# Value products of an attention pair grouped one stage later, and the operands of TensorE gathered at the low SBUF addresses

## The chip, the cores and the metric

One core of a Trainium2 chip runs the whole program: TensorE for matmuls, VectorE (DVE), ScalarE (ACT) and GpSimd (POOL) for the rest, SyncE (SP) for the queue of most transfers. The metric is the device time of one execution in microseconds, here the median of three runs.

## What is computed

A network of three blocks over a sequence of 512 positions and 1024 features, in float32:

```python
a = rmsnorm(h, g); q, k, v, u, z = split(a @ w_in)
h = h + rmsnorm(concat(norm(dilated_attention(q, k, v)), norm(gating(u, z))) @ w_out, g)   # 8 heads
h = h + rmsnorm((silu(f @ w_gate) * (f @ w_up)) @ w_down, g)                              # 2816 wide
h = h + sigmoid(h @ w_pe_gate + b) * (p @ w_pe_proj)
for i in range(2):
    h = rms_norm(x) * (1 + sc1) + sh1
    mix = stick_breaking_attention(h) if i == 0 else dsa_attention(h)                     # 16 heads each
    x = x + g1 * mix
    x = x + g2 * conv_ffn(rms_norm(x) * (1 + sc2) + sh2)                                  # 2816 wide
```

All three attentions end alike: a 512 x 512 matrix of weights per head, lower triangle only, times the head's values (512 x 64). `dsa_attention` first picks 128 keys per query by an index score.

## The kernel before

Activations are kept feature-major: 128 features on the partitions, 512 positions along the row, so a tensor of 1024 features is eight tiles of 128 x 512. Every large product is made of three: each operand is rounded to a `float32r` high part and a low part that holds the remainder, and `mm3` (L103) adds low weights x high operand, high weights x high operand, high weights x low operand into one PSUM bank. `unit` (L82) loads 128 x 1024 weights into `raw` and rounds them into two pairs `whi`, `wlo` (ScalarE casts, VectorE subtracts); the streamed operands are `hh`/`hl` (normed activations), `mh`/`ml`, `q` or `k` (attention outputs before their projection) and `Hh`/`Hl` (22 tiles each, the inner layer of a feed-forward part). In a product of 128 x 128 weights and a 128 x 512 operand the operand is the moving one; only the values (`tokmajor`) do it the other way round.

The program runs in order: the dilated mixer with its gating (`mixer_a`), a feed-forward part with a gate (`ffn_a`), stick-breaking attention (`mixer_sb`), a feed-forward part (`ffn_conv`), sparse attention (`mixer_dsa`), a second `ffn_conv`.

Attention is written out by hand in `attend` (L522). It goes through pairs of heads, 4 in the first part and 8 in each of the other two, with one stage per pair. In stage i it issues eight `block`s (scores and weights of pair i+1, one for each head and block of 128 queries) and, for pair i, `tr` after every second block and `mul` behind it; between them it takes a number of steps from `filler`, a generator of float32r products that have nothing to do with the pair (projections to come). While `order` is on, TensorE runs its instructions exactly in the order written (`queue`, L71).

`av` (L636) makes the three functions of a pair. `tr(kb)` turns the weights of key block kb, 128 columns at a time, into the PSUM tile `tt` (one buffer), and copies it to `AT` (two buffers). `mul(kb)` multiplies it with the values `v`, for both heads, into bank `po` (one buffer), in full float32 on 64 columns of the array: four records in the profile. In the stage, `mul(kb-1)` follows `tr(kb)`, and `mul(3)` and `end` close it. `end` rounds `po` into the operand of the output projection (`ms`).

SBUF tiles live in pools that are laid out one behind the other from the low end: `const`, `w` (raw, whi, wlo, ada), `x` (X, hh, hl), `small` (acc, sq, R and others, 8608 bytes), then the pools of the stage that runs. A tile takes its size rounded up to 32 bytes per partition.

Of the kernel before, what the change touches and what calls it, by code (L numbers as in the profile page):

```python
# [8 lines left out]
F32 = mybir.dt.float32  # L9
F32R = mybir.dt.float32r  # L10
# [44 lines left out]


class K:
    def __init__(self, tc, a, stop=99):
# [5 lines left out]
    def t(self, pool, shape, dt=F32, tag="t", bufs=None):  # L64
        self.n += 1
        return pool.tile(list(shape), dt, name=f"{tag}_{self.n}", tag=tag, bufs=bufs)


# [18 lines left out]
    def unit(self, src, widths=(512, 512), eng=None):  # L87

        nc = self.nc
        n, raw = sum(widths), src  # L90
        if src is not self.first:
            raw = self.t(self.wp, [P, UNIT], F32, "raw", bufs=4)
            nc.sync.dma_start(raw[:, :n], src[:, :n])
        out, c = [], 0
        for w in widths:
            hi = self.t(self.wp, [P, 512], F32R, "whi", bufs=7)
            lo = self.t(self.wp, [P, 512], F32R, "wlo", bufs=7)
            nc.scalar.copy(hi[:, :w], raw[:, c:c + w])  # L98
# [11 lines left out]
    def units(self, srcs):  # L110

        nc = self.nc
        raws, out = [], [[] for _ in srcs]
        for src in srcs:
            raws.append(self.t(self.wp, [P, UNIT], F32, "raw", bufs=4))
            nc.sync.dma_start(raws[-1], src)
        for j in range(2):
            for raw, o in zip(raws, out):
                hi = self.t(self.wp, [P, 512], F32R, "whi", bufs=7)
                lo = self.t(self.wp, [P, 512], F32R, "wlo", bufs=7)  # L120
# [149 lines left out]
    def build(self):  # L270
        tc, nc, a = self.tc, self.nc, self.a
        with ExitStack() as ctx:
            cp = ctx.enter_context(tc.tile_pool(name="const", bufs=1))
            self.wp = ctx.enter_context(tc.tile_pool(name="w", bufs=1))
            self.xp = ctx.enter_context(tc.tile_pool(name="x", bufs=1))
            self.sp = ctx.enter_context(tc.tile_pool(name="small", bufs=1))
            self.dp = ctx.enter_context(tc.tile_pool(name="dram", bufs=1, space=bass.MemoryType.DRAM))
            self.pp = ctx.enter_context(tc.tile_pool(name="banks", bufs=1, space=PSUM))
            self.cp = cp

            X = [self.t(self.xp, [P, S], F32, f"X{k}") for k in range(KD)]
            self.consts = self.t(cp, [P, NCOLS], F32, "consts")
# [7 lines left out]
            self.order(False)  # L290
            self.ident = self.t(cp, [P, P], F32, "ident")
            nc.gpsimd.memset(self.ident, 0.0)
# [43 lines left out]
    def mixer_a(self, X, raw):  # L336
# [9 lines left out]
        with ExitStack() as ctx:  # L346
            mp = ctx.enter_context(tc.tile_pool(name="mixa", bufs=1))
            gctx = ctx.enter_context(ExitStack())
# [108 lines left out]

            def av(i, A):
                o, tr, mul = self.av(at, A, lambda kb, h: V[kb][:, (2 * i + h) * 64:(2 * i + h + 1) * 64], nc.scalar.copy)

                def end():
                    if i < 2:
# [60 lines left out]
    def attend(self, pairs, block, av, filler, budget, ahead=0):  # L523

        A = None
        self.order(True)
        for _ in range(ahead):  # L530
            next(filler, None)
        for i in range(-1, pairs):
            nxt, n = [[], []], budget[i + 1]
            share = (0, 2, 3, 4, 5, 6, 7, 8, 9)
            if i >= 0:
                tr, mul, end = av(i, A)
            for s in range(8):
# [12 lines left out]
        for _ in filler:  # L550
            pass
        self.order(False)

# [81 lines left out]

    def av(self, pool, A, V, copy):  # L636

        nc = self.nc  # L640
        out, at = self.bank("po"), {}
# [13 lines left out]

        def mul(kb):
            for h in range(2):
                self.matmul(out[h * 64:h * 64 + 64, kb * P:], V(kb, h), at[kb][:, h, :S - kb * P], start=kb == 0, stop=kb == NB - 1)

# [232 lines left out]
    def mixer_sb(self, X):  # L892
        tc, nc, a = self.tc, self.nc, self.a
        with tc.tile_pool(name="sb", bufs=1) as mp:
            w = a["sb_w_in"]
            slab, operand = self.enter(X, 0, [w[8 + i] for i in range(4)])
            identb = self.t(mp, [P, P], BF16, "identb")
            nc.vector.tensor_copy(identb, self.ident)
            dmask = self.t(mp, [P, S], F32, "keep", bufs=2)[:, :P]
            nc.vector.memset(dmask, 0.0)  # L900
# [27 lines left out]
            def block(h, qb):  # L928
# [15 lines left out]
            def av(i, A):  # L944
                o, tr, mul = self.av(mp, A, lambda kb, h: V[kb][:, (2 * i + h) * 64:(2 * i + h + 1) * 64], None if i == 7 else nc.vector.tensor_copy)

                def end():
                    if i < 6:
                        ms.append(self.split(o, i, "m", mp))
                        return  # L950
# [26 lines left out]
    def ffn_conv(self, X, l):  # L977
        tc, nc, a = self.tc, self.nc, self.a
        with tc.tile_pool(name="ffn", bufs=1) as fp:
            w = a["ffn_w_up"][l]  # L980
# [32 lines left out]
    def mixer_dsa(self, X):  # L1013
        tc, nc, a = self.tc, self.nc, self.a
        with ExitStack() as ctx:
            Tw = self.Tw
            mp = ctx.enter_context(tc.tile_pool(name="dsa", bufs=1))
            w = a["dsa_w_in"]
# [24 lines left out]
            self.slabs([pk[:72]], [self.unit(w[5], (288, 288))], xs, m=72)  # L1043
            ki = self.t(mp, [P, 1, 2, S], F32R, "AT", bufs=2)
            for h in range(2):
# [88 lines left out]
            def ahead():  # L1134
# [16 lines left out]
                nc.vector.tensor_mul(gg, self.col("dsa_q_norm"), self.col("dsa_k_norm"))  # L1151
                kn.append(self.t(mp, [P, S], F32, "kn"))
                nc.vector.scalar_tensor_tensor(kn[0], lat, gg, Rk, op0=ALU.mult, op1=ALU.mult)
# [83 lines left out]
            def av(i, A):  # L1237
                o, tr, mul = self.av(mp, A, lambda kb, h: V[kb][:, (2 * i + h) * 64:(2 * i + h + 1) * 64], nc.scalar.copy)

                def end():  # L1240
                    hi = self.t(mp, [P, S], F32R, f"q{2 * i}")
                    lo = self.t(mp, [P, S], F32R, f"q{2 * i + 1}")
# [23 lines left out]
    def rel_bias(self, pool):  # L1266
# [3 lines left out]
        nc.gpsimd.dma_start(rb, a["rel_bias"])  # L1270
        row = self.t(pool, [P, 2, S], F32, "AT", bufs=2).rearrange("p a b -> p (a b)")[:DH]
        b = t5_buckets()
# [101 lines left out]
```

## Time and profile before

| | us |
|---|---|
| median of three runs | 1953.95 (1952.02 to 1954.26) |
| the profiled execution | 1953.02 |
| its span | 1951.3 |
| TensorE busy | 1912.0 |
| VectorE busy | 1297.6 |
| ScalarE busy | 906.4 |
| GpSimd busy | 366.4 |

The span runs from the first to the last instruction. Busy times of one engine count overlapping records once. Matmuls are pipelined, so that a record of TensorE is longer than the time by which it delays the next one; the distance between two starts tells that. A granted clock of 1.00 is TensorE's upper level, 2.4 GHz. Names such as `mm<-hh,wlo` are the tile written and the two tiles read.

### The profile page before, as it was taken

The numbers are of one execution on the slowest core, as the hardware profiler recorded it, in microseconds if no ns is written. First come the engines' busy times: TensorE is split into PE (matmuls) and PEld (weight loads), VectorE is DVE, ScalarE is ACT, GpSimd is POOL, SyncE is SP. The second block draws the span as 40 slices with busy tenths as digits, with TensorE's granted clock in tenths as the row PEclk, the third lists the DMA queues.
The fourth block names the chain that finished last, engine by engine and source line by source line (L and its number), as shares of the span: only waits on it lengthen the run. The fifth ranks groups of instructions, "written<-read, shape, count | busy, mean of one in ns | idle before, by whom it ended". The sixth has DMA issues, their size and how long they took to land.

```text
span 1951.3 us, 24100 instructions
## 1 busy us (share of the span) xinstructions
PE 1912.0 (98%) x8610; PEld 1504.1 (77%) x8610; DVE 1297.6 (66%) x2354; ACT 906.4 (46%) x1672; POOL 366.4 (19%) x348
## 2 busy tenths in 40 slices
PE   7999799999999999999999999999999999999999
PEld 6887678888887787767888888886665688888887
DVE  6686775556356666776888874568967677666431
ACT  5365443223324455554544443345588655444321
POOL 3020331111000302332111110013454221111000
PEclk8999899999999999999999999999999999999999
DMA  5232156555464243222366555522212123322331
GB/s 181 87 89 69 62 170 188 192 184 177 144 219 148 79 129 87 76 63 81 105 204 198 196 170 167 212 92 98 81 60 65 33 89 119 97 98 95 94 108 49
DMA packets 70382, 236.93 MB, mean 121 GB/s; under 512 B 8085, under 2 KB 8677, under 8 KB 70262
## 3 DMA queue, kind: packets, MB, share of 16 engines
q1 hardware_dynamic: 69556, 234.47, 37.4%
q8 instruction: 67, 1.10, 0.2%
q10 hardware_dynamic: 578, 0.85, 0.2%
q14 instruction: 53, 0.43, 0.1%
q0 software_dynamic: 128, 0.08, 0.0%
HBM read 226.87 MB, written 2.21 MB: 117 GB/s over the span
## 4 chain that ended last, share of the span: by engine, by line
PE 88%; DVE 8%; issue 2%; ACT 1%; POOL 1%; DMA 0%; SPq 0%; POOLq 0%; DVEq 0%; ACTq 0%
PE mm L81 52%; PE sc L81 27%; PE po L81 5%; PE tt L84 2%; PE tt L81 1%; DVE isc L1093 1%; DVE m L1092 1%; DVE hl L262 1%; DVE wlo L99 0%; DVE hh L589 0%; DVE X L590 0%; DVE g L739 0%; DVE wlo L123 0%; DVE hl L852 0%; DVE v L1030 0%
## 5 line engine op out<-in xcount | busy, mean ns | idle before, releaser
L98 ACT CAST whi<-raw 128x512 fp32r<-128x512 f32 (+1 forms) x550 | 327.5, 607 | 423.5 <-PE mm L81 248.9
L99 DVE TENSOR_TENSOR wlo<-raw,whi 128x512 fp32r<-128x512 f32 (+1 forms) x518 | 381.6, 745 | 206.2 <-ACT whi L98 201.8
L81 PE MATMUL mm<-hh,wlo 128*128 128x512 f32 (+1 forms) x1000 | 406.4, 406 | 3.5 <-ACT hh L261 3.5
L81 PE MATMUL mm<-hl,whi 128*128 128x512 f32 x1032 | 402.1, 393 | 0.0
L81 PE MATMUL mm<-hh,whi 128*128 128x512 f32 (+1 forms) x1000 | 391.9, 392 | 0.0
L81 PEld LDWEIGHTS mm<-hh,wlo 128*128 128x128 f32 (+1 forms) x1000 | 188.6, 189 | 70.9 <-issue 30.3
L81 PEld LDWEIGHTS mm<-hl,whi 128*128 128x128 f32 x1032 | 194.4, 188 | 42.3
L767 DVE CUSTOM_DVE_ANT_0 ada<-ada,bc 128x1024 f32<-128x1024 f32 x112 | 139.8, 1248 | 124.0 <-DMA ada<-in_ada_w 96.5
L81 PEld LDWEIGHTS mm<-hh,whi 128*128 128x128 f32 (+1 forms) x1000 | 188.7, 189 | 36.4 <-issue 0.8
L81 PE MATMUL sc<-hh,wlo 128*128 128x512 f32 x416 | 162.5, 391 | 0.0
L81 PE MATMUL sc<-hl,whi 128*128 128x512 f32 x416 | 162.3, 390 | 0.0
L81 PE MATMUL sc<-hh,whi 128*128 128x512 f32 x416 | 162.3, 390 | 0.0
L190 POOL TENSOR_TENSOR acc<-acc,sq 128x512 f32<-128x512 f32 x53 | 84.9, 1601 | 407.1 <-ACT sq L195 399.5
L81 PE MATMUL mm<-Hl,whi 128*128 128x512 f32 x364 | 144.3, 397 | 0.0
L81 PE MATMUL mm<-Hh,wlo 128*128 128x512 f32 x364 | 144.1, 396 | 0.0
L81 PE MATMUL mm<-Hh,whi 128*128 128x512 f32 x364 | 143.6, 395 | 0.0
L1004 POOL TENSOR_TENSOR g<-g,u 128x512 f32<-128x512 f32 x44 | 62.6, 1422 | 413.5 <-DVE u L1000 358.6
L252 ACT CAST Hh<-g 128x512 fp32r<-128x512 f32 x66 | 41.0, 621 | 164.3 <-POOL g L691 100.7
L81 PEld LDWEIGHTS sc<-hh,wlo 128*128 128x128 f32 x416 | 78.5, 189 | 16.3
L81 PEld LDWEIGHTS sc<-hh,whi 128*128 128x128 f32 x416 | 78.4, 189 | 16.3
L81 PEld LDWEIGHTS sc<-hl,whi 128*128 128x128 f32 x416 | 78.4, 188 | 16.3
L81 PE MATMUL sc<-Hl,whi 128*128 128x512 f32 x220 | 87.4, 397 | 0.0
(364 smaller groups left out, 3356.0 us busy)
## 6 DMA issues: line engine op xcount, KB each, us to landing
ada<-in_ada_w SPq DMA_DIRECT2D x96, 512.0 KB, 4.0
raw<-in_ffn_w_up SPq DMA_DIRECT2D x88, 512.0 KB, 3.2
raw<-in_w_gate_up SPq DMA_DIRECT2D x44, 512.0 KB, 4.3
raw<-in_ffn_w_down SPq DMA_DIRECT2D x32, 512.0 KB, 3.5
raw<-in_sb_w_in SPq DMA_DIRECT2D x24, 512.0 KB, 3.2
raw<-in_dsa_w_in SPq DMA_DIRECT2D x21, 512.0 KB, 3.4
raw<-in_w_in SPq DMA_DIRECT2D x19, 512.0 KB, 3.3
raw<-in_w_down SPq DMA_DIRECT2D x16, 512.0 KB, 4.1
```

Of the source, the lines that this page charges most:

```text
L81: self.queue(self.nc.tensor.matmul(*args, **kw))
L84: self.queue(self.nc.tensor.transpose(*args))
L98: nc.scalar.copy(hi[:, :w], raw[:, c:c + w])
L99: (eng or nc.vector).tensor_sub(lo[:, :w], raw[:, c:c + w], hi[:, :w].bitcast(F32))
L190: (eng or self.nc.gpsimd).tensor_add(acc, acc, self.square(src))
L252: self.nc.scalar.copy(hi, src)
L262: self.nc.vector.scalar_tensor_tensor(lo, src, col, hi.bitcast(F32), op0=ALU.mult, op1=ALU.subtract)
L767: nc.vector.tensor_tensor_reduce(raw, raw, row, scale=1.0, scalar=0.0, op0=ALU.mult, op1=ALU.add, accum_out=out))
L1004: nc.gpsimd.tensor_mul(g, g, u)
L1092: nc.vector.max(m8, work[qb][:, :L])
L1093: nc.vector.match_replace(work[qb][:, :L], m8, work[qb][:, :L], SENT)
```

## The change

Five things change.

`attend` no longer issues `mul` and `end` in the stage of their pair. It keeps them as `late` and issues all four `mul` and `end` in the next stage, behind its first block; those of the last pair come behind the rest of the filler. `tr` stays where it was. `AT` becomes four tiles, one per key block and of its size; in the dilated part the one of 256 columns borrows the tile `bc`. The bank `po` is taken at `mul(0)`.

Pools get a side. From the low end come `unit` (ident), `wt` (whi, wlo) and `x` (hh, hl); from the high end `const`, `w` (raw, ada), `res` (the residual X) and `small`. A stage's pool becomes two (`Homes`): the tags named go to the low side, all others to the high side. Low are the operands `mh`/`ml`, `qs`, `k` in the dilated and stick-breaking parts, `q` and the `v` tags in the sparse part, and in the feed-forward parts all `Hh` and `Hl8` to `Hl11`.

`norms` in the sparse part squares two heads at a time and issues their two products together, with one copy instead of two.

`keep` in the stick-breaking part uses the tiles `R` and `acc` in turn instead of two of its own; `kn` in the sparse part uses `acc`.

The tile for the mask, the index keys and the bias row is `AT512` instead of `AT`.

```diff
+class Homes:
+    def tile(self, shape, dt, name, tag, bufs=None):
+        return (self.low if tag in self.tags else self.high).tile(shape, dt, name=name, tag=tag, bufs=bufs)
...
+    @contextmanager
+    def homes(self, name, tags):
+        with self.tc.tile_pool(name=name, bufs=1) as low, self.tc.tile_pool(name=name + "_", bufs=1, side="right") as high:
+            yield Homes(low, high, tags)
...
-            hi = self.t(self.wp, [P, 512], F32R, "whi", bufs=7)
-            lo = self.t(self.wp, [P, 512], F32R, "wlo", bufs=7)
+            hi = self.t(self.wt, [P, 512], F32R, "whi", bufs=7)
+            lo = self.t(self.wt, [P, 512], F32R, "wlo", bufs=7)
...
-            cp = ctx.enter_context(tc.tile_pool(name="const", bufs=1))
-            self.wp = ctx.enter_context(tc.tile_pool(name="w", bufs=1))
+            self.ip = ctx.enter_context(tc.tile_pool(name="unit", bufs=1))
+            self.wt = ctx.enter_context(tc.tile_pool(name="wt", bufs=1))
             self.xp = ctx.enter_context(tc.tile_pool(name="x", bufs=1))
-            self.sp = ctx.enter_context(tc.tile_pool(name="small", bufs=1))
+            cp = ctx.enter_context(tc.tile_pool(name="const", bufs=1, side="right"))
+            self.wp = ctx.enter_context(tc.tile_pool(name="w", bufs=1, side="right"))
+            self.rp = ctx.enter_context(tc.tile_pool(name="res", bufs=1, side="right"))
+            self.sp = ctx.enter_context(tc.tile_pool(name="small", bufs=1, side="right"))
...
-            mp = ctx.enter_context(tc.tile_pool(name="mixa", bufs=1))
+            mp = ctx.enter_context(self.homes("mixa", [f"m{p}{i}" for p in "hl" for i in range(8)]))
...
-            at = ctx.enter_context(tc.tile_pool(name="atta", bufs=1))
+            at = ctx.enter_context(self.homes("atta", ("qs0", "qs1", "k")))
...
-        A = None
+        A, late = None, None
...
+                if s == 0 and late is not None:
+                    for kb in range(NB):
+                        late[0](kb)
+                    late[1]()
                 if i >= 0 and s % 2:
                     tr(s // 2)
-                    if s > 1:
-                        mul(s // 2 - 1)
...
             if i >= 0:
-                mul(NB - 1)
-                end()
+                late = mul, end
...
+        for kb in range(NB):
+            late[0](kb)
+        late[1]()
...
-            at[kb] = self.t(pool, [P, 2, S], F32, "AT", bufs=2)
+            if n == 256 and spare:
+                at[kb] = self.t(self.cp, [P, D], F32, "bc", bufs=1)[:, :2 * n].rearrange("p (h n) -> p h n", h=2)
+            else:
+                at[kb] = self.t(pool, [P, 2, n], F32, f"AT{n}", bufs=1)
...
-        with tc.tile_pool(name="ffn", bufs=1) as fp:
+        with self.homes("ffn", [f"Hh{i}" for i in range(KF)] + [f"Hl{i}" for i in range(8, 12)]) as fp:
...
-        with tc.tile_pool(name="sb", bufs=1) as mp:
+        with self.homes("sb", [f"m{p}{i}" for p in "hl" for i in range(8)] + ["qs0", "qs1", "k"]) as mp:
...
-                keep = self.t(mp, [P, S], F32, "keep", bufs=2)
+                keep = self.t(self.sp, [P, S], F32, ("R", "acc")[qb % 2], bufs=1)
...
-            mp = ctx.enter_context(tc.tile_pool(name="dsa", bufs=1))
+            mp = ctx.enter_context(self.homes("dsa", [f"q{i}" for i in range(16)] + [f"v{i}" for i in range(4)]))
...
-                for j in range(n):
-                    sq = self.square(Q[h - n + 1 + j])
+                for j in range(0, n, 2):
+                    sqs = [self.square(Q[h - n + 1 + j + i]) for i in range(2)]
                     yield
-                    pn, js = self.sc_ps(), slice(j * 32, (j + 1) * 32)
-                    self.matmul(pn[js], ones32, sq, start=True, stop=True)
+                    yield
+                    pn = self.sc_ps()
+                    for i in range(2):
+                        self.matmul(pn[(j + i) * 32:(j + i + 1) * 32], ones32, sqs[i], start=True, stop=True)
+                    js = slice(j * 32, (j + 2) * 32)
                     nc.scalar.copy(rows[js], pn[js])
```

## Rows read from the trace of the kernel before

**Rows 1.** The page: busy time, share and instructions; the chain that ended last.
```profile
PE 1912.0 (98%) x8610; PEld 1504.1 (77%) x8610; DVE 1297.6 (66%) x2354; ACT 906.4 (46%) x1672; POOL 366.4 (19%) x348
...
PE 88%; DVE 8%; issue 2%; ACT 1%; POOL 1%; DMA 0%; SPq 0%; POOLq 0%; DVEq 0%; ACTq 0%
```

**Rows 2.** Waits of TensorE: total us, times, longest us.
```profile
PE tt L81 <- POOL rc L229: 9.1, 4, 4.8
...
PE po L81 <- ACT AT L654: 0.2, 1, 0.2
```

**Rows 3.** Windows: stick-breaking stages, sparse stages, index rounds; length, then busy (instructions).
```profile
754.00:886.30 132.30, 132.30 (x713) 92.97 (x711) 102.65 (x134) 69.92 (x160) 43.50 (x54) 1.00 0.24 71
1428.90:1549.20 120.30, 119.22 (x559) 71.70 (x558) 85.36 (x329) 101.11 (x227) 50.91 (x55) 1.00 0.19 60
1352.00:1412.00 60.00, 57.07 (x239) 39.44 (x238) 59.69 (x172) 30.35 (x55) 27.28 (x26) 1.00 0.21 68
```

**Rows 4.** Timeline of TensorE, transposes without a `mul`: start, us, instruction.
```profile
789.76 0.94 PE L84 MATMUL tt<-ident,A 128*128 128x128 f32 x7
...
790.87 0.39 PE L81 MATMUL mm<-hh,whi 128*128 128x512 f32 x1
```

**Rows 5.** Timeline of TensorE, transposes with `mul(0)`; neighbouring windows.
```profile
794.86 0.38 PE L84 MATMUL tt<-ident,A 128*128 128x128 f32 x2
795.17 0.65 PE L81 MATMUL po<-AT,v 128*64 128x512 f32 x2
795.65 0.60 PE L81 MATMUL po<-AT,v 128*64 128x512 f32 x2
...
796.51 0.40 PE L81 MATMUL mm<-hh,whi 128*128 128x512 f32 x1
```

**Rows 6.** Timeline of TensorE around a `mul(3)` between float32r products.
```profile
785.52 0.40 PE L81 MATMUL mm<-hl,whi 128*128 128x512 f32 x1
...
786.57 0.23 PE L81 MATMUL sc<-dmaskb,identb 128*128 128x128 bf16 x1
```

**Rows 7.** Timeline behind the last value product of the stick-breaking part, three engines.
```profile
895.23 0.50 PE L81 MATMUL mm<-k,wlo 128*128 128x512 f32 x1
...
895.37 0.59 ACT L952 CAST k<-po 128x512 fp32r<-128x512 f32 x1 [1.66 <-PE po L81]
...
895.99 0.69 DVE L953 TENSOR_TENSOR k<-po,k 128x512 fp32r<-128x512 f32 x1 [2.91 <-ACT k L952]
```

**Rows 8.** Timeline of a copy out of `tt` and TensorE's next transposes.
```profile
872.95 0.93 DVE L654 COPY AT<-tt 128x768 f32<-128x768 f32 x1
...
874.09 0.39 PE L81 MATMUL sc<-k,qs 128*128 128x256 f32 x2
874.32 0.23 PE L81 MATMUL sc<-dmaskb,identb 128*128 128x128 bf16 x1
874.39 0.39 PE L84 MATMUL tt<-ident,A 128*128 128x128 f32 x2
```

**Rows 9.** Timeline of TensorE around one sum-of-squares product.
```profile
1474.54 1.04 PE L81 MATMUL sc<-sq,ones 128*32 128x512 f32 x2
...
1475.86 0.39 PE L81 MATMUL mm<-hh,whi 128*128 128x512 f32 x1
```

**Rows 10.** The chain in order of time: `hh`, `Hh` and `q` streaming; start, us.
```profile
978.41 16.32 PE mm L81 x72
...
1225.09 30.80 PE sc L81 x132
...
1560.46 23.77 PE mm L81 x102
```

**Rows 11.** Groups by form: busy us, mean ns; `hh` 932:1162, `q6`/`q7` 1562.81:1563.02, `q8` on 1563.5:1564.9.
```profile
L81 PE MATMUL mm<-hh,wlo 128*128 128x512 f32 x202 | 78.7, 389 | 0.0
...
L81 PE MATMUL mm<-q,whi 128*128 128x512 f32 x2 | 0.6, 389 | 0.0
...
L81 PE MATMUL mm<-q,whi 128*128 128x512 f32 x5 | 1.7, 397 | 0.0
L81 PE MATMUL mm<-q,wlo 128*128 128x512 f32 x2 | 0.8, 393 | 0.0
```

More of the change, by code (lines that the diff above doesn't have):

```diff
@@ L2 @@
 import math
-from contextlib import ExitStack
+from contextlib import ExitStack, contextmanager
 import concourse.bass as bass
@@ L54, in t5_buckets, with __init__ @@
     return out
+class Homes:
+    def __init__(self, low, high, tags):
+        self.low, self.high, self.tags = low, high, tags
+    def tile(self, shape, dt, name, tag, bufs=None):
+        return (self.low if tag in self.tags else self.high).tile(shape, dt, name=name, tag=tag, bufs=bufs)
 class K:
@@ L118, in units @@
             for raw, o in zip(raws, out):
-                hi = self.t(self.wp, [P, 512], F32R, "whi", bufs=7)
-                lo = self.t(self.wp, [P, 512], F32R, "wlo", bufs=7)
+                hi = self.t(self.wt, [P, 512], F32R, "whi", bufs=7)
+                lo = self.t(self.wt, [P, 512], F32R, "wlo", bufs=7)
                 part = raw[:, j * 512:(j + 1) * 512]
@@ L279, in build @@
             self.cp = cp
-            X = [self.t(self.xp, [P, S], F32, f"X{k}") for k in range(KD)]
+            X = [self.t(self.rp, [P, S], F32, f"X{k}") for k in range(KD)]
             self.consts = self.t(cp, [P, NCOLS], F32, "consts")
@@ L290, in build @@
             self.order(False)
-            self.ident = self.t(cp, [P, P], F32, "ident")
+            self.ident = self.t(self.ip, [P, P], F32, "ident")
             nc.gpsimd.memset(self.ident, 0.0)
@@ L458, in av @@
             def av(i, A):
-                o, tr, mul = self.av(at, A, lambda kb, h: V[kb][:, (2 * i + h) * 64:(2 * i + h + 1) * 64], nc.scalar.copy)
+                out, tr, mul = self.av(at, A, lambda kb, h: V[kb][:, (2 * i + h) * 64:(2 * i + h + 1) * 64], nc.scalar.copy, True)
                 def end():
+                    o = out[0]
                     if i < 2:
@@ L634, in softmax, with av @@
         return e
-    def av(self, pool, A, V, copy):
+    def av(self, pool, A, V, copy, spare=False):
         nc = self.nc
-        out, at = self.bank("po"), {}
+        out, at = [], {}
         def tr(kb):
@@ L656, in mul @@
         def mul(kb):
+            if kb == 0:
+                out.append(self.bank("po"))
             for h in range(2):
-                self.matmul(out[h * 64:h * 64 + 64, kb * P:], V(kb, h), at[kb][:, h, :S - kb * P], start=kb == 0, stop=kb == NB - 1)
+                self.matmul(out[0][h * 64:h * 64 + 64, kb * P:], V(kb, h), at[kb][:, h, :S - kb * P], start=kb == 0, stop=kb == NB - 1)
         return out, tr, mul
@@ L898, in mixer_sb @@
             nc.vector.tensor_copy(identb, self.ident)
-            dmask = self.t(mp, [P, S], F32, "keep", bufs=2)[:, :P]
+            dmask = self.t(mp, [P, 2, S], F32, "AT512", bufs=1)[:, 0, :P]
             nc.vector.memset(dmask, 0.0)
@@ L944, in av @@
             def av(i, A):
-                o, tr, mul = self.av(mp, A, lambda kb, h: V[kb][:, (2 * i + h) * 64:(2 * i + h + 1) * 64], None if i == 7 else nc.vector.tensor_copy)
+                out, tr, mul = self.av(mp, A, lambda kb, h: V[kb][:, (2 * i + h) * 64:(2 * i + h + 1) * 64], None if i == 7 else nc.vector.tensor_copy)
                 def end():
+                    o = out[0]
                     if i < 6:
@@ L978, in ffn_conv @@
         tc, nc, a = self.tc, self.nc, self.a
-        with tc.tile_pool(name="ffn", bufs=1) as fp:
+        with self.homes("ffn", [f"Hh{i}" for i in range(KF)] + [f"Hl{i}" for i in range(8, 12)]) as fp:
             w = a["ffn_w_up"][l]
@@ L1043, in mixer_dsa @@
             self.slabs([pk[:72]], [self.unit(w[5], (288, 288))], xs, m=72)
-            ki = self.t(mp, [P, 1, 2, S], F32R, "AT", bufs=2)
+            ki = self.t(mp, [P, 1, 2, S], F32R, "AT512", bufs=1)
             for h in range(2):
@@ L1151, in ahead @@
                 nc.vector.tensor_mul(gg, self.col("dsa_q_norm"), self.col("dsa_k_norm"))
-                kn.append(self.t(mp, [P, S], F32, "kn"))
+                kn.append(self.t(self.sp, [P, S], F32, "acc", bufs=1))
                 nc.vector.scalar_tensor_tensor(kn[0], lat, gg, Rk, op0=ALU.mult, op1=ALU.mult)
@@ L1237, in av @@
             def av(i, A):
-                o, tr, mul = self.av(mp, A, lambda kb, h: V[kb][:, (2 * i + h) * 64:(2 * i + h + 1) * 64], nc.scalar.copy)
+                out, tr, mul = self.av(mp, A, lambda kb, h: V[kb][:, (2 * i + h) * 64:(2 * i + h + 1) * 64], nc.scalar.copy)
                 def end():
+                    o = out[0]
                     hi = self.t(mp, [P, S], F32R, f"q{2 * i}")
@@ L1270, in rel_bias @@
         nc.gpsimd.dma_start(rb, a["rel_bias"])
-        row = self.t(pool, [P, 2, S], F32, "AT", bufs=2).rearrange("p a b -> p (a b)")[:DH]
+        row = self.t(pool, [P, 2, S], F32, "AT512", bufs=1).rearrange("p a b -> p (a b)")[:DH]
         b = t5_buckets()
```

## The prediction

> **What bounds the kernel now.** The page comes first. TensorE is busy in 98% of the span, and the chain that ended last runs 88% of the way over its matmuls [rows 1]. So a change pays only in so far as it shortens TensorE's own stream or removes one of its few waits. Of these the view of the waits shows little: nine kinds, the largest 9.1 us behind GpSimd's `rc`, and of the value products only one wait of 0.2 us behind the copy they read [rows 2]. The windows over the attention parts then say that TensorE has no gap in the stick-breaking part and 1.1 us of gaps in the sparse one, where ScalarE is busy 101 of 120 us [rows 3]. In one stretch, 1352 to 1412, VectorE is the engine without a gap; what TensorE saves there is worth nothing. TensorE's records overlap, so its cost is read from the distance between the starts of neighbours, not from the duration of one. The profiled execution took 1953.0 us, with a span of 1951.3; the median of the three runs is 0.9 us above it. The sum is made against 1953.0 and 0.9 is added at the end.
>
> **Part 1, the value products of a pair in one group.** A pair has four `tr` (8, 6, 4 and 2 transposes) and four `mul` (two products of full float32, 64 columns wide). Today `mul(kb-1)` follows `tr(kb)`, and `mul(3)` stands alone at the stage's end: four excursions out of the float32r stream. What one costs is read so. Eight transposes alone take from 789.76 to the second float32r product behind them at 790.87: 1.11, less 0.23 for the first product (its price: [rows 10]), is 0.88, or 0.11 a transpose with the way out of them included [rows 4]. With a `mul` behind: two transposes from 794.86, then four records of 512 columns, then the second float32r product at 796.51. Of these 1.65 us, 0.22 are the transposes, 0.85 the columns (2048 at the granted 2.4 GHz) and 0.23 a float32r product; 0.35 is overhead [rows 5]. `mul(3)` between float32r products: 785.52 to 786.57 is 1.05, less 0.23, 0.21 of columns and 0.23 for the two 256-column products (874.09 to 874.32), 0.38 [rows 6, 8]. Of it 0.10 stands in front, 0.05 between the two heads (the first from 795.17 to 795.65, 0.48 for 0.43 of columns), and the rest behind [rows 5].
>
> After the change the eight products stand together behind the first block of the next stage. Entry and exit are paid once, the step between products eight times: 0.26 + 8 x 0.05 = 0.66, against 3 x 0.35 + 0.38 = 1.43; I take a little less than the difference, 0.73 a pair, and with 4 + 8 + 8 pairs **14.6 us**. The step from the second head of one key block to the first head of the next isn't in the trace. Its lower bound is the 0.05 between the heads, its upper bound a whole exit and entry, which would leave nothing of the gain; I take 0.05, since the same kind of product stands on both sides in that row.
>
> Nothing but matmuls moves on TensorE; `end()` moves too, with a ScalarE cast, a VectorE subtraction and, in the dilated part, a GpSimd add per pair, and no transfer. Its readers, the output projection's early steps, use a pair's result a stage or more later, except for the last pair. There the filler is now spent before the products, so TensorE meets `ms[7]` empty-handed: today the next product starts at 895.23, the cast runs from 895.37 to 895.96 and the subtraction from 895.99 to 896.68, hidden by six products of the filler [rows 7]. Uncovered, TensorE waits from 895.23 to about 896.0, runs two products and waits again for the low half: 0.8 + 0.25 = 1.05 in each of two parts. In the dilated part three other operands come first and only `norm_cols(aacc)` may be early, some 0.4. **2.5 us lost.**
>
> The transposes share one PSUM bank, `tt`. `tr(kb+1)` waits for the copy of `tr(kb)`, and the `mul` that lay between was cover, 1.2 or 1.0 us of it. In one stage the copy runs from 872.95 to 873.88; the next `tr` comes at 874.39 and would come 1.2 earlier [rows 8]: 0.7 of waiting. Bounds: nothing (the queue is emptier while eight products run) and 0.7 for ten tight gaps, 7 us; I take **1.5 us lost**, two or three such places.
>
> **Part 2, norms two at a time.** A sum-of-squares product and the float32r product behind it take 1.32 (1474.54 to 1475.86); less 0.85 for two records of 512 columns in full float32 (0.43 each, as above) and 0.23, it is 0.24 [rows 9]. Pairing removes 8 of 16 excursions at 0.24, 2 us; half fall into VectorE's stretch and are worth nothing. **1.0 us gained.**
>
> **Part 3, placement.** Two long runs of the same float32r product, same `whi`/`wlo` weights and same PSUM tags: with `hh`/`hl` streaming, 72 take 16.32 us, 226.7 ns each; with `Hh`/`Hl`, 132 take 30.80, 233.3 ns; the sparse output projection, 102 of `q` in 23.77, 233.0 [rows 10]. What differs is where the operand lies. Adding up the tile sizes, `hh`/`hl` start between 88,320 and 119,040 bytes at multiples of 128; the stage pools begin at 129,696, 32 bytes past one, because the small pool is 8608 bytes, and their operands start 32, 64 or 96 past. Distance or alignment? In the sparse projection `q5`, `q6` and `q7` happen to sit at 200,704, 202,752 and 204,800, multiples of 128 and far up. Fast runs have a mark in the records, a mean of 389 ns (`hh`); the aligned pair of `q` shows 389 too, the misaligned ones behind it 393 and 397 [rows 11]. That speaks for alignment and against height.
>
> The change puts ident, the weights and the operands (512, 28,672 and 32,768 bytes) at the bottom, then the stage's operands; all are multiples of 128, so everything in the low pools starts right. The shared high pools take 5760, 20,480, 16,384 and 8608 bytes from the top, 229,376, and end at 178,144, 96 past a multiple; below that 18 of 22 `Hl` stay. In a projection of the feed-forward parts, 4 triples gain 3 x 6.7 ns and 18 triples, two right and one wrong, gain between 0 (the wrong one upsets its neighbours) and 13; I take 6: 24 x (80 + 108) = 4.5 us. The gate projection, half and half, 0.8. The attention output projections run long and undisturbed: 1.0 each in two parts, 0.4 in the first. Short runs inside attention gain perhaps 2 ns each, 0.6. **8.3 us**, bounds 4 and 12. What else moves (residual, raw weights, masks), and `keep` and `kn` with as many tiles in turn as before, is read by engines with slack; cover gone, it would show first on ScalarE in the sparse part [rows 3].
>
> A page of the Trainium skill speaks against this part: "SBUF — State Buffer", Specifications (TRN2), has operands read in lines of 16 bytes. Every tile here starts on a multiple of 32, so by that rule neither the old places nor the new ones could differ, and the sum would lose its 8.3 us. The trace disagrees by the 6 to 7 ns a product of [rows 10], unless something other than the place makes them, which is the first rival.
>
> **The sum.** -14.6 - 1.0 - 8.3 + 2.5 + 1.5 = -19.9; 1953.0 - 19.9 + 0.9 = **1934**.
>
> **Rivals.**
> *Placement is nothing*: `hh` and `Hh` differ by something else, such as the length of an accumulation. For it: a projection sums 22 blocks, an up-projection 8. Against: `q` sums 8 and is slow except where aligned [rows 10, 11]. 1934 + 8.3 = 1942. This is also what "the low tiles aren't aligned after all" gives.
> *Each value product pays for itself*: the group costs what four groups did. Against: the 0.05 between heads [rows 5]. 1934 + 14.6 = 1949.
> *More than summed*: mixed triples gain the full 13 ns (3 us more), the waits at the ends and at `tt` don't come (4 us): 1927.
> *Slower*: the turnaround of `tt` becomes the bound. TensorE loses whatever the copy takes beyond the work between two `tr`. That work shrinks to some 2.8 us in the mean: a stage of the sparse part, 120.3 / 7 = 17.2 us [rows 3], less 0.7, the group's 2.8 and 20 transposes of 0.11, by four; the copy shown ends 0.5 before the next `tr` [rows 8]. With three gaps in each of 20 pairs, every 0.35 us beyond the mean costs 21 us: from a mean turnaround of 3.15 on, the kernel is slower, 1958 at 3.2. For it: ScalarE is busy 84% in the sparse part, and the eight products squeeze its eight blocks into less time. Against: without the group the next `tr` still has a block and a filler step before it.
>
> **How the numbers follow.** Forecast 0.55, its own range 1928 to 1940. Placement nothing 0.14, products pay each 0.08, more than summed 0.18, slower 0.05 (of which 0.03 beyond 0.2%). A measurement tells some 0.2%, 4 us, from no change. Faster by more: 0.55 + 0.14 + 0.18 + most of 0.08 = 0.93; same 0.04; slower 0.03. The range takes the forecast with placement's bounds and half of the products' case: 1926 to 1944.
>
> **What would show it.** Right: 80 groups of value products become 20, of 16 records; a transpose is followed by float32r at 0.03; inside a group, starts 0.05 beyond their columns. Triples of `Hh`, `Hh`, `Hl` in the down-projections below 0.70, and 0.68 where `Hl8` to `Hl11` stand; output projections at 227 ns. New waits of TensorE behind the cast of the last pair, near 0.8. Wrong: steps of 0.26 between key blocks; `Hh` still at 233; waits of transposes behind the `AT` copies in every pair.

## The result, and the profile after

The changed kernel takes 1925.05 us (median; 1919.95 to 1927.14), the kernel before, run beside it, 1954.11: a ratio of 0.985, 95% interval 0.983 to 0.987. That is 29.1 us gained where 19.9 were forecast, and just outside the range, 1926 to 1944. The profiled execution took 1926.12 us with a span of 1924.4; its answer to [rows 1], from the page:

```profile
PE 1877.1 (98%) x8610; PEld 1508.7 (78%) x8610; DVE 1289.8 (67%) x2354; ACT 897.7 (47%) x1664; POOL 372.8 (19%) x348
...
PE 77%; DVE 6%; issue 2%; ACT 1%; POOL 0%; POOLq 0%; DVEq 0%; ACTq 0%
```

TensorE's busy time falls by 34.9 us, the span by 26.9. Both numbers of instructions of TensorE are as before; the same products stand closer. The 8 us between the two are waits that are new or have grown. The waits of TensorE after (engine, what waits, what for; total us, times, longest), to be set beside [rows 2]:

```profile
PE tt L95 <- POOL rc L243: 9.4, 4, 5.2
...
PE sc L95 <- DVE nm L1264: 6.2, 1, 6.2
...
PE tt L98 <- DVE AT L681: 0.7, 2, 0.6
PE tt L95 <- POOL acc L204: 0.7, 1, 0.7
PE mm L95 <- ACT k L982: 0.7, 1, 0.7
PE mm L95 <- ACT q L1277: 0.7, 1, 0.7
...
PE tt L98 <- ACT AT L681: 0.4, 2, 0.2
```

The waits behind `k`, `q` and `acc` are those forecast at the ends of the three attention parts, the four behind `AT` (two rows) those forecast at `tt`. The wait behind `nm` was 3.9 us in two before and is 6.2 in one now, and the two small ones behind `sq` are gone. In the view of before they stood so:

```profile
PE sc L81 <- DVE nm L1231: 3.9, 2, 3.0
...
PE sc L81 <- ACT sq L195: 0.9, 2, 0.4
```

The 6.2 us are the end of the stretch in which VectorE is the engine without a gap [rows 3]. The windows around it (length, then busy time of PE, PEld, DVE, ACT, POOL; granted clock, DMA share, GB/s):

```profile
1390.00:1397.00 7.00, 1.01 (x5) 0.50 (x3) 6.66 (x15) 1.38 (x2) 6.14 (x8) 0.71 0.11 29
1397.00:1414.00 17.00, 16.57 (x58) 11.65 (x59) 11.96 (x52) 12.98 (x33) 7.17 (x9) 0.82 0.13 44
```

TensorE stands still while VectorE is busy for 6.66 of 7 us, and the clock in the 17 us behind it is granted at 0.82 in the mean: part of the 17 us ran at the lower level, 1.2 GHz. What TensorE saves ahead of that point comes back here as waiting.

A group of eight value products, TensorE's timeline of a stick-breaking stage (start, us, instruction; the row x16 merges all eight products, two records each; the first record alone lasts 0.64), to be set beside [rows 5, 6]:

```profile
817.44 0.23 PE L95 MATMUL sc<-dmaskb,identb 128*128 128x128 bf16 x1
817.60 2.37 PE L95 MATMUL po<-AT,v 128*64 128x512 f32 x16
819.91 0.50 PE L95 MATMUL mm<-hh,wlo 128*128 128x512 f32 x1
820.25 0.39 PE L95 MATMUL mm<-hh,whi 128*128 128x512 f32 x1
```

From 817.60 to 819.91 are 2.31 us, 2.13 of them columns (1280 for each head, the two heads together, four times over at 2.4 GHz). The sixteen records start in eight pairs, one record of each head, 7 ns apart; the two x2 rows of [rows 5] are such pairs as well (two records of 0.64 in 0.65). So the two heads of a key block run at the same time, each in two passes, and the step that the prediction calls one between two heads is the step from the first pass to the second. From pair to pair, and from the last to the next product, it is 480, 429, 322, 323, 216, 215, 110 and 209 ns. The first of these holds 0.05 above its 427 of columns and the last 0.10; the six between are columns alone. The next float32r product adds 0.11 (0.34 for 0.23), and the instruction in front some 0.09. So the group costs about 0.36 above its columns, as one group of a single key block did.

This isn't the price of full float32 as such. The scores of the sparse part are full float32 too, but on all 128 columns of the array; in the kernel before, between the same float32r products:

```profile
1492.63 0.39 PE L81 MATMUL mm<-hl,whi 128*128 128x512 f32 x1
1492.86 0.81 PE L81 MATMUL sc<-kn,q 128*128 128x384 f32 x2
...
1493.73 0.39 PE L81 MATMUL mm<-hh,whi 128*128 128x512 f32 x1
```

The product in front takes its 0.23, and from 1492.86 to 1493.73 are 0.87: 0.64 of columns and 0.23 for the first float32r product, so the way in and out costs 0.01 at most. The value products and the sums of squares differ from these by their 64 and 32 columns; what it is in a narrow product that costs isn't shown.

Two sums of squares, timeline of TensorE, to be set beside [rows 9]:

```profile
1376.59 0.39 PE L95 MATMUL mm<-hl,whi 128*128 128x512 f32 x1
1376.91 1.05 PE L95 MATMUL sc<-sq,ones 128*32 128x512 f32 x4
1377.89 0.50 PE L95 MATMUL mm<-hh,wlo 128*128 128x512 f32 x1
1378.23 0.39 PE L95 MATMUL mm<-hh,whi 128*128 128x512 f32 x1
```

Two products take 0.98 us together, from 1376.91 to 1377.89. One alone took 0.98 before, from 1474.54 [rows 9] to the next product:

```profile
1475.52 0.50 PE L81 MATMUL mm<-hh,wlo 128*128 128x512 f32 x1
```

The row of [rows 9] has two records in 1.04, this one four in 1.05. They run at the same time on different columns of the array.

The long runs of [rows 10], from the chain in order of time after (start, us, engine, tile, line, count), and two groups by form (busy us, mean ns):

```profile
1213.79 30.52 PE sc L95 x132
...
1535.18 23.12 PE mm L95 x102
```

```profile
L95 PE MATMUL mm<-Hh,whi 128*128 128x512 f32 x364 | 143.0, 393 | 0.0
L95 PE MATMUL mm<-Hl,whi 128*128 128x512 f32 x364 | 143.0, 393 | 0.0
```

`q` now runs at 226.7 ns a product (23.12 / 102) instead of 233.0; `Hh`/`Hl` at 231.2 (30.52 / 132) instead of 233.3.

### The profile page after: what moved, and what is told of

The parts are those of the page before. It is cut to its first block, busy times and chain, and to the rows that moved or that the text cites. A ratio compares the mean times of both kernels' runs of the same rounds, so it can differ in the third digit from the quotient of the medians.

```text
span 1924.4 us, 24081 instructions
## 1 busy us (share of the span) xinstructions
PE 1877.1 (98%) x8610; PEld 1508.7 (78%) x8610; DVE 1289.8 (67%) x2354; ACT 897.7 (47%) x1664; POOL 372.8 (19%) x348
## 4 chain that ended last, share of the span: by engine, by line
PE 77%; DVE 6%; issue 2%; ACT 1%; POOL 0%; POOLq 0%; DVEq 0%; ACTq 0%
PE mm L95 45%; PE sc L95 26%; PE po L95 3%; PE tt L98 2%; PE tt L95 1%; DVE isc L1123 1%; DVE m L1122 1%; DVE hl L276 0%; DVE g L768 0%; DVE hl L881 0%; DVE v L1060 0%; DVE rst L223 0%; DVE isc L1103 0%; DVE q L879 0%; DVE wlo L113 0%
## 5 line engine op out<-in xcount | busy, mean ns | idle before, releaser
L204 POOL TENSOR_TENSOR acc<-acc,sq 128x512 f32<-128x512 f32 x53 | 89.5, 1688 | 394.8 <-ACT sq L209 387.2
L95 PEld LDWEIGHTS sc<-hh,wlo 128*128 128x128 f32 x416 | 78.7, 189 | 16.3
L95 PEld LDWEIGHTS sc<-hh,whi 128*128 128x128 f32 x416 | 78.6, 189 | 16.3
L95 PE MATMUL sc<-Hh,wlo 128*128 128x512 f32 x220 | 86.7, 394 | 0.0
```

The costliest lines, as they stand in the source:

```text
L95: self.queue(self.nc.tensor.matmul(*args, **kw))
L204: (eng or self.nc.gpsimd).tensor_add(acc, acc, self.square(src))
```

## The experiments

**Each part alone.** Three kernels carry one part of the change each. For the grouping, the pools stay on one side and in the old order and `norms` stays as it was; `AT` by sizes and the new homes of `keep` and `kn` come with it, since `AT` needs the room:

```
-                    if s > 1:
-                        mul(s // 2 - 1)
...
+                if s == 0 and late is not None:
+                    for kb in range(NB):
+                        late[0](kb)
+                    late[1]()
```

> Grouping alone: the value products of a pair together one stage later, places and norms as before. Theory A (from the rows of after: inside a group the starts of neighbours lie 480, 429, 322, 323, 216, 215, 110, 209 ns apart, so way in and way out cost about 0.36 us once and a step inside costs nothing): 3 x 0.355 = 1.07 us a pair, 21.3 us for 20 pairs, less some 2.5 us of new waits, so 1935. Rival B (the prediction's 0.05 for each of eight steps): 14.6 less 4.0, so 1943.5.

Measured: 1939.16 us against 1954.27, ratio 0.9925 (0.9907 to 0.9944): 15 us gained, 11 to 18 by the interval. It lies between the two numbers, and neither is within the interval, so the trace has to tell. From the first transpose of one pair to that of the next, the stages changed by (us, after less before):

```
dilated:          -1.08 -1.09 -1.04
stick-breaking:   -1.07 -1.12 -1.05 -1.09 -1.16 -0.32 -0.24
sparse:           -1.30 -1.28 -0.03 -1.03 -0.53 -0.79 -1.03
```

Ten of the seventeen stages gain theory A's 1.07 to within 0.1, and none of the undisturbed ones gains as little as B's 0.73. Five gain less than 1.07, by 3.4 us together, and two gain more, by 0.4 together. For one of the five, the last of the stick-breaking part, a reason stands in this kernel's timeline:

```profile
865.05 0.23 PE L95 MATMUL sc<-dmaskb,identb 128*128 128x128 bf16 x1
865.84 0.66 PE L98 MATMUL tt<-ident,A 128*128 128x128 f32 x4 [0.56 <-DVE AT L678]
```

So the sum of the part alone is 20 x 1.07 = 21.4, less 3.0 in these stages, less 2.1 of waits at the ends (0.7 each behind `k`, `q` and `acc`, in this kernel's waits too): 16.3, inside the interval. The view of the waits names 1.0 of the 3.0 as waiting behind `AT`; the rest shows as longer ways to and from the transposes of the same stages, and its cause stays open.

For the norms, only the loop of `norms` is taken over:

```
-                for j in range(n):
-                    sq = self.square(Q[h - n + 1 + j])
...
+                for j in range(0, n, 2):
+                    sqs = [self.square(Q[h - n + 1 + j + i]) for i in range(2)]
...
```

> Norms two at a time alone. Theory A (two sum-of-squares products on different 32-column positions run side by side when they stand together): about 0.9 us of TensorE's stream for each of eight pairs, 7.2 in all; half of it (the first four pairs) lies beside VectorE's stretch 1352 to 1412 and may be worth nothing: 1947 to 1950.5. Rival B (only eight ways in and out saved, as predicted): 1953.

Measured: 1946.74, ratio 0.9963 (0.995 to 0.9976): 7.5 us gained, 5 to 10 by the interval. B falls. By the starts in the trace, counted from the first product of the program, the first block of sparse attention begins 6.0 us earlier than before and its first transposes only 2.0 earlier; the last value product comes 6.8 earlier. So 4.0 us are given back ahead of the attention, and in it 4.8 are gained, about what its four pairs make (4 x 1.16 = 4.6, below). With the small waits that go, 0.9 us behind `sq` and 0.9 of those behind `nm`, the 9.3 of eight pairs less the 4.0 make 7.1, for 6.8. The windows where it is given back, and the wait of that kernel:

```profile
1390.00:1400.00 10.00, 10.00 (x44) 6.56 (x45) 10.00 (x33) 4.98 (x9) 3.01 (x3) 1.00 0.16 52
1400.00:1410.00 10.00, 4.02 (x19) 3.04 (x17) 9.65 (x26) 2.39 (x3) 6.50 (x8) 0.90 0.08 24
```

```profile
PE sc L81 <- DVE nm L1234: 6.1, 1, 6.1
```

For the placement, the pools get their sides and the stages their two homes, and nothing else changes:

```
-            cp = ctx.enter_context(tc.tile_pool(name="const", bufs=1))
-            self.wp = ctx.enter_context(tc.tile_pool(name="w", bufs=1))
+            self.ip = ctx.enter_context(tc.tile_pool(name="unit", bufs=1))
+            self.wt = ctx.enter_context(tc.tile_pool(name="wt", bufs=1))
...
-        with tc.tile_pool(name="ffn", bufs=1) as fp:
+        with self.homes("ffn", [f"Hh{i}" for i in range(KF)] + [f"Hl{i}" for i in range(8, 12)]) as fp:
...
```

> Placement alone, products and norms as before. Theory A (a moving operand that starts on a multiple of 128 bytes runs at 227 ns, one that does not at 233): Hh, q, mh and the queries and keys gain, Hl0 to 7 and Hl12 to 21 do not: 4 to 8 us, 1946 to 1950. Rival C (the place does nothing): 1954, the means of Hh and Hl stay at 233 ns.

Measured: 1945.42, ratio 0.9956 (0.994 to 0.9971): 8.9 us gained, 6 to 12 by the interval. Rival C falls. The three parts alone give 15.1 + 7.5 + 8.9 = 31.5, the whole change 29.1; with intervals of some 3 us each they add up.

**Is it alignment, and to what?** First the kernel before, with its operands as high up as they were, and 96 bytes of padding in the small pool:

```
+            self.t(self.sp, [P, 24], F32, "pad")
...
-            cc = self.t(fp, [P, 4, 44], F32, "conv")
+            cc = self.t(fp, [P, 4, 48], F32, "conv")[:, :, :44]
```

> The kernel before with 96 bytes more in the small pool, and the convolution's table padded from 704 to 768 bytes: every Hh and Hl starts on a multiple of 128, as high up as before. Alignment theory: 1776 products of the down and gate projections at 227 instead of 233 ns, 144 of the 192 products of q likewise, 11 to 13 us: 1942. Rival (low addresses are what is fast): no change, 1954, Hh still at 233 ns.

Measured: 1942.98, ratio 0.9939 (0.9919 to 0.9958). Height is out. The same run as in [rows 10], and the means, in this kernel:

```profile
1221.95 29.92 PE sc L81 x132
```

```profile
L81 PE MATMUL mm<-Hl,whi 128*128 128x512 f32 x364 | 141.6, 389 | 0.0
L81 PE MATMUL mm<-Hh,whi 128*128 128x512 f32 x364 | 141.6, 389 | 0.0
```

29.92 / 132 is 226.7 ns, the speed of `hh` and `hl`, and the 389 ns of [rows 11] is there. Then the counter-test, the kernel after with everything low moved by 32 bytes:

```
             self.ip = ctx.enter_context(tc.tile_pool(name="unit", bufs=1))
+            self.t(self.ip, [P, 8], F32, "pad")
             self.wt = ctx.enter_context(tc.tile_pool(name="wt", bufs=1))
```

> The kernel after with 32 bytes more at the very bottom, so that rounded weights, hh and hl and every low operand start 32 past a multiple of 128, as low as before. Alignment theory: some 4400 products of hh and hl and some 2300 of the other low operands go from 227 to 231 to 234 ns: 25 to 45 us slower, 1950 to 1970; the mean of hh goes from 389 to 393 to 397 ns. Rival (low addresses are what is fast): 1925, hh still at 227 ns.

Measured: 1926.82, ratio 0.9866 (0.9847 to 0.9885). The alignment theory as it stood falls: 4400 products stream from addresses 32 bytes past a multiple of 128, and a run of 72 of them takes what it took in [rows 10]:

```profile
283.47 16.32 PE mm L95 x72
...
1219.22 30.51 PE sc L95 x132
```

A theory for both runs: what counts isn't where the operand starts but whether it starts as far past a multiple as its weights do. In the last run both had moved together; in the kernel before the weights were on multiples, so that the two theories said the same. The test moves the weights by 32 bytes and everything else that is low by 128, which for the alignment to 128 is nothing:

```
             self.ip = ctx.enter_context(tc.tile_pool(name="unit", bufs=1))
+            self.t(self.ip, [P, 8], F32, "pad")
             self.wt = ctx.enter_context(tc.tile_pool(name="wt", bufs=1))
             self.xp = ctx.enter_context(tc.tile_pool(name="x", bufs=1))
+            self.t(self.xp, [P, 24], F32, "pad")
```

> The kernel after with 32 bytes in front of the rounded weights and 96 behind them, so that the weights alone lie 32 past a multiple of 128, and hh, hl and the low operands on multiples as before. Theory D (a product is fast where its moving operand and its weights lie equally far past a multiple of 128): nearly every wide float32r product goes from 227 to 232 to 235 ns, some 4900 of them by 6 and the 1400 of mixed triples by 2 to 3: 30 to 36 us slower, 1955 to 1961. Rival E (the operand's own place, or the weights' being on a multiple, decides; moving everything by 32 cost nothing, so this should not either): 1925 to 1927.

Measured: 1956.00, ratio to the kernel before 1.0011 (1.0001 to 1.002): 31 us above the kernel after, which is D. Every run of 72 has gone from 16.32 to 16.80, 233.3 ns a product:

```profile
286.27 16.80 PE mm L95 x72
314.27 16.80 PE mm L95 x72
```

```profile
L95 PE MATMUL mm<-hh,whi 128*128 128x512 f32 x992 | 393.1, 396 | 0.0
```

That the 128 bytes of the operands aren't harmless by themselves comes out of the next run. The weights' place counts all the same: by the tile sizes `hh` starts at 45,824 here and at 88,320 in the kernel before, both on a multiple of 256, slow here and fast there. What differs is the weights, 160 bytes past such a multiple here (17,056) and on one there (39,168).

How far must the two agree? The aligned kernel before again, with 224 bytes of padding instead of 96:

```
-            self.t(self.sp, [P, 24], F32, "pad")
+            self.t(self.sp, [P, 56], F32, "pad")
```

> As the aligned kernel before, but with 224 bytes more in the small pool instead of 96: Hh and Hl lie 128 past the place of the weights modulo 256. If agreement modulo 128 is what counts: Hh and Hl at 227 ns, 1943 as the aligned one. If agreement modulo 256 is needed: Hh and Hl at 232 to 235 ns, 1953.

Measured: 1954.02, ratio 1.0002 (0.9993 to 1.0012); all of the aligned kernel's gain is gone.

```profile
1223.45 30.68 PE sc L81 x132
```

30.68 / 132 is 232.4 ns. Agreement modulo 128 isn't enough. Modulo 512 isn't needed: in the aligned kernel before, the weights start at 39,168 (256 past a multiple of 512) and `Hh` at 130,560 (0 past one), and that pair is fast. So the modulus is 256, by all pairs of places that these runs have.

Last, the part that the change left out, the `Hl` that stay high, 64 bytes out of step with the weights: the kernel after with 64 bytes of padding in the small pool and the table of the convolution padded as above.

> The kernel after with 64 bytes more in the small pool and the convolution's table padded to 768 bytes, so that the Hl that stay high start on multiples of 128 too. Alignment theory: 1776 products of Hh and Hl go from 231 to 227 ns: 7 us faster, 1918. Rival (low is what counts): 1925.

Measured: 1921.67, ratio 0.9829 (0.9815 to 0.9844), and once more, beside the kernel after:

> The kernel after, beside the aligned one on the same chip: 1925, as before.

> The aligned kernel after. If the starts in the trace carry over to the time: 7 us below the kernel after, 1918. If something gives part of it back: 1921 to 1923.

1924.38 (0.9852, 0.9837 to 0.9868) and 1918.99 (0.9827, 0.981 to 0.9844): the medians are 5.4 us apart. The intervals overlap, so that the whole time leaves the gain likely and not proved; the trace is plain:

```profile
1208.80 29.92 PE sc L95 x132
...
1528.55 23.12 PE mm L95 x102
```

Much of what the profiled executions differ by lies near 600 us, ahead of the stick-breaking attention: there TensorE waits for `acc` for 0.7 us and not at all in the two of the kernel after, 1.2 and 1.8 in the two of the aligned one, and 3.9 to 5.1 in three kernels below that differ from these only behind that point. From the first transposes of the stick-breaking part to TensorE's end the two profiled executions of the kernel after take 1174.76 and 1174.79 us, those of the aligned one 1169.49 and 1169.50. So the padding gains 5.3 us there.

**Do sums of squares run side by side?** The kernel after with both products of a pair on columns 0 to 31, each in its own bank, and copied one by one:

```
-                    pn = self.sc_ps()
+                    pns = [self.sc_ps() for i in range(2)]
                     for i in range(2):
-                        self.matmul(pn[(j + i) * 32:(j + i + 1) * 32], ones32, sqs[i], start=True, stop=True)
+                        self.matmul(pns[i][:32], ones32, sqs[i], start=True, stop=True)
...
```

> The kernel after with the two sum-of-squares products of a pair on the same 32 columns, each in a bank of its own, one behind the other as before. Theory A (they run side by side because they are on different columns): a pair takes 1.85 us instead of 0.98, some 7 us slower over eight pairs less what VectorE's stretch hides, 1928.5 to 1932. Rival (it is the saved way in and out): the pair still takes 0.98 us, 1925.

Measured: 1929.02, ratio 0.9874 (0.9859 to 0.9888). The pair stands together as before, and takes 1.83 us (1345.38 to 1347.21) instead of 0.98:

```profile
1345.38 1.91 PE L95 MATMUL sc<-sq,ones 128*32 128x512 f32 x4
1347.21 0.50 PE L95 MATMUL mm<-hh,wlo 128*128 128x512 f32 x1
```

So it is the columns, not the company. And four of them on four positions, in the first two groups:

```
+                g = 4 if h < 8 else 2
+                for j in range(0, n, g):
+                    sqs = [self.square(Q[h - n + 1 + j + i], None if i < 2 else self.t(mp, [P, S], F32, "sb", bufs=4)) for i in range(g)]
...
```

> The kernel after with the first eight sums of squares in two groups of four, on four different positions of 32 columns. If four run side by side as two do: a group takes about 1.0 us plus 0.2, two groups of four save two times 1.2, 2.4 us of TensorE's stream, all of it in VectorE's stretch: between 1922.5 and 1925. Rival (only two run side by side): a group of four takes 1.9 us, 1925.

Measured: 1925.89, ratio 0.9854 (0.9838 to 0.987): no gain in the time, as the rival has it, but not for the rival's reason. Four products take 1.00 us, 1349.49 to 1350.48:

```profile
1349.49 0.62 PE L95 MATMUL sc<-sq,ones 128*32 128x512 f32 x2
1349.50 0.62 PE L95 MATMUL sc<-sb,ones 128*32 128x512 f32 x2
1349.94 0.60 PE L95 MATMUL sc<-sq,ones 128*32 128x512 f32 x2
1349.95 0.60 PE L95 MATMUL sc<-sb,ones 128*32 128x512 f32 x2
1350.48 0.50 PE L95 MATMUL mm<-hh,wlo 128*128 128x512 f32 x1
```

What is saved lies in VectorE's stretch and turns into waiting: that kernel's waits have a second one there, 3.6 us behind `qms`, beside 6.3 behind `nm`.

**Can that waiting be filled?** The aligned kernel after, with the projection of one more query in the index stretch and one less in the attention:

```
-                for h in range(5, 10):
+                for h in range(5, 11):
...
-            self.attend(DH // 2, block, av, filler(), (8, 11, 8, 9, 9, 7, 6, 9, 7))
+            self.attend(DH // 2, block, av, filler(), (7, 10, 7, 8, 8, 6, 5, 8, 6))
```

> The aligned kernel after (e_all), with the projection of query 10 moved from the attention stages into the index stretch, where TensorE waits 6.2 us for VectorE and then runs 10 us at half clock. Theory: the wait is filled by 5.6 us of products that are wanted anyway: 5 to 9 us faster than e_all's 1921.7, 1913 to 1917. Rival (VectorE or ScalarE bounds what is behind, so the attention part gains nothing): 1920 to 1922.

Measured: 1922.53, ratio 0.9843 (0.9828 to 0.9858): nothing gained; the rival holds. The filling itself works: the sparse part's first transposes come 522.17 us after the last value product of the stick-breaking part, for 521.92 in the aligned kernel, with 21 products more in that time, and the wait behind `nm` falls from 6.2 to 3.7. But the attention behind, with these 21 products less (4.8 us at 226.7 ns), takes as long as before, 120.5 us from its first transposes to its last value product against 120.8. Both kernels need 642.7 us for the two together. TensorE has 3.0 us of gaps in it now, for 0.5. The windows of that stretch, this kernel's and then the aligned one's:

```profile
1409.76:1530.31 120.55, 117.56 (x601) 77.46 (x600) 87.62 (x346) 101.15 (x235) 51.04 (x56) 1.00 0.18 53
1403.79:1524.57 120.78, 120.30 (x622) 81.35 (x621) 85.02 (x342) 101.89 (x236) 54.51 (x59) 1.00 0.20 62
```

Of the gaps 1.6 us stand behind `AT` (0.4 in the aligned kernel) and 0.8 behind `nm`. Which of the two other engines holds the attention isn't shown.

And with the groups of four added:

> As the run with query 10 moved, and the first eight sums of squares in two groups of four. Four products on four column positions take 996 ns together in the earlier run, where two took 983: another 2.3 us off TensorE's stream. If the moved query covers the wait: 1911 to 1915, 0 to 2 us below that run. Rival: VectorE still holds the stretch and the 2.3 us are given back: the same time as that run.

Measured: 1923.30, ratio 0.9845 (0.983 to 0.986): the same time, within the noise; its wait behind `nm` is 7.7 us. VectorE holds the stretch.

## Why the prediction was wrong, and where it was right

**The value products, mis-sized by 7 us.** The step that failed is "the step between products eight times: 0.26 + 8 x 0.05". The 0.05 was read at 795.65 [rows 5] as a step between the two heads. It isn't one, since the heads run at the same time: it is the step from the first pass of both to their second. And it is the one place in a group where 0.05 stands: the first step of eight has it too, and the six behind it have none. It belongs to the way in. With 0.36 a group whatever its length, a pair saves 1.43 - 0.36 = 1.07 and not 0.73; 20 pairs save 21.4, not 14.6. The rows shown before had only groups of one key block, with one such step, so a price by step and a price by entry couldn't be told apart there; the second should have been an end of the range.

**The norms, mis-sized by 6.5 us.** "Pairing removes 8 of 16 excursions at 0.24" counts the way in and out, and misses that half of the columns go. The rows had it: in [rows 5] a value product of 512 columns, 64 wide, takes 0.43 in a pair, and in [rows 9] one of 512 columns, 32 wide, stands alone and takes 0.85. The prediction used both numbers and didn't ask why one is half of the other: the two heads stand on different columns and run together, a lone sum of squares has no partner. A pair of sums took 2 x 1.17 before (0.98, and some 0.09 and 0.10 around it) and takes 1.18 now, 1.16 saved; eight pairs make 9.3, and 7.5 came. That products on different columns of the array run at the same time stands in the Trainium skill, "TensorE: Matmul & The Clock Gate", Part 3: Packing small matmuls; its table in "Why this matters for your kernels" gives 2.38 times for three of 32 columns. The trace agrees: 0.98 us for one, 0.98 for two, 1.00 for four. The other half of the step, that what falls into VectorE's stretch is worth nothing, was right in kind: of 6.0 us, 4.0 came back as waiting.

**The placement, right in size, half right in mechanism.** 8.3 forecast, 8.9 measured alone. Against height and against chance the argument from `q6` and `q7` [rows 11] held. But "multiples of 128" isn't the rule. A wide float32r product takes 226.7 ns where moving operand and weights start equally far past a multiple of 256 bytes, and 232 to 235 where they don't. The forecast came out because all that it called aligned also agreed modulo 256; `q5` to `q7` and the rounded weights of the kernel before did. That was luck, since nothing in it looked at where the weights lie. The `Hl` that stay high are 64 bytes out of step and not the 96 that its sum gives, since 64 bytes of padding put them right. The mixed triples gained a little less than was taken: 30.80 to 30.52 for 44 triples is 6.4 ns each in the mean, where 4 in 22 at 20 and 18 at 6 would have made 8.5. All three products of a mixed triple are slow, not the odd one alone. The rule on lines of 16 bytes in "SBUF — State Buffer", Specifications (TRN2), of the Trainium skill, gives no reason why a shift by 32 or 128 bytes should matter. The 31 us that the run with shifted weights lost show that it isn't the whole rule; the measurement decides.

**The waits.** At the ends 2.5 was forecast and 2.1 came (0.7 each behind `k`, `q` and `acc`; the second wait for the low half didn't). At `tt` 1.5 was forecast in two or three places; the waits name 1.0, and the five stages that gain less lost 3.4. "Slower" by the turnaround of `tt` did not come: nine of the fourteen stages in the two later parts lost nothing.

**Of the rivals**, "more than summed" named nearly the right time, 1927, for the wrong reasons: the waits it left out came, and the mixed triples didn't gain in full. Two terms that no rival held made the rest.

The range failed for one reason: both mis-sized terms were read at one or two places of the trace; the first had its bounds only on the side of a smaller gain, the second had none.

## What to carry to other kernels

Before a narrow product is costed, compare its time per column with every other narrow product in the trace: where one takes half, ask what runs beside it, and put the lone ones together on different columns. Place moving operand and weights equally far past a multiple of 256 bytes; a tile of odd size early in a pool moves all that lies behind it, and 64 bytes of padding can be worth 5 us. And a gain on an engine that another one holds up a little later is worth nothing until that one is faster; filling its wait with work from elsewhere pays only if elsewhere is bound by the same engine.

## What the runs showed of the hardware that was not expected

- A wide float32r product depends on where weights and moving operand lie relative to each other, modulo 256 bytes: 226.7 ns or 232 to 235. Both moved by 32 bytes: 16.32 us for 72; the weights by 32 and the operands by 128: 16.80.
- One operand out of step slows its two neighbours too: in runs of two right and one wrong, all three have starts 231 to 233 ns apart.
- Four full-float32 products of 512 columns on four positions of 32 take 1.00 us, one alone 0.98.
- The way from float32r products to value products on 64 columns and back costs about 0.36 us, for one key block or for all four; to full float32 scores on 128 columns and back, 0.01.
